# Low-query passes on 128 rows instead of 64, in two attentions and a memory attention

## The chip, the cores and the metric

The kernel runs on 1 core of a Trainium2 chip. The metric is device time in microseconds (us) of one execution; lower is better. TensorE (PE) multiplies: its weight loads are told as PEld and overlap with its matmuls. VectorE (DVE), ScalarE (ACT) and GpSimd (POOL) do the rest; SyncE (SP) issues every DMA here.

## The reference

A trunk of two layers on a sequence of 1024 positions of width 1024, all in float32. Cut to what the change touches:

```python
for layer in range(2):
    h = rms_norm(x, mix_norm_g[layer])
    da_q, da_k, da_v, sb_q, sb_k, sb_v, c_q, c_kv, k_r = split(h @ w_in[layer])
    y_a = diff_attention(...)     # 4 heads; per head two softmaxes over 64-wide q and k, plus a bias
    y_b = stick_breaking(...)     # 4 heads of 64
    y_c = latent_attention(...)   # 4 heads of 64 + 32
    x = x + concatenate([y_a, y_b, y_c]) @ w_out[layer]
    x = x + memory_attention(rms_norm(x), mem, ...)   # 4 heads of 64 over 256 memory tokens
    x = x + square(relu(rms_norm(x) @ w_ff1[layer])) @ w_ff2[layer]
```

In each of these attentions the scores of a head are `q @ k.T`, with q and k 64 wide (96 in the latent attention), and masked so that a query sees its own block and those before it.

## The kernel before

*Precision.* Matmuls run in a reduced float32 (`F32R`). An operand is therefore split into a high part (rounded to that format) and a low part (what is left), and a product is made of passes: high x high, high x low, low x high. In the projections, `mm3` (L572 to L575) issues three matmuls for each block.

*Rows.* A matmul sums over rows, at most 128. Where a head is 64 wide, two of those passes fit in one matmul: the keys' tile `ks` has the high keys in rows 0 to 63 and the low keys in rows 64 to 127 (`stack`, L961), and the queries' tile `qh` has the high queries twice (`twice`, L975). One pass of 128 rows so gives high x high + high x low. The low queries `ql` lie on 64 rows (`block`, L969), and the second pass takes rows 0 to 63 of both: low x high. Latent heads (96 wide) have three passes of 96 or 100 rows.

*Attention.* `attention(h, ...)` (L940) does one half of the queries: h = 0 are the tiles 0 to 3 of 128 queries, with up to 512 keys; h = 1 are the tiles 4 to 7, with up to 1024. For each of the 4 heads of a kind, the tiles of queries and keys are loaded from scratch in DRAM by `dma` on SP's queue, then for each tile of queries `scores` (L989) issues the passes: each over the keys in pieces of at most 512 columns, one bank of PSUM. Half 0 has one piece a pass (PSUM tile `e`), half 1 has two (PSUM tile `d`). In a differential head (`da_head`, L1066) there are two such score blocks a tile of queries, and each has two more matmuls that add the bias through a permutation (`flip`). Query tiles and biases share the ring of tiles named `o` (6 or 7 of them), keys are in `kst`, values in `v`. After the scores come a row maximum (L1091), exponentials, or sigmoids and a scan (L1121) in the stick-breaking heads, transposes through PE (L594) and the products with the values (L1027, L1042, L1044).

*Memory attention.* It is part of `merge` (L1156), once for each half of the queries and each layer. Its keys `km` are stacked high over low on 128 rows; the queries, transposed and present on both halves of the rows, are split into `qT[:, 0]` (high, L1188) and `qT[:64, 1]` (low, L1189). For each of 4 heads there is one pass of 128 rows (L1200) and one of 64 (L1201), 256 columns each.

*Order.* The program isn't run as written. `order_engines` (L223) plans all of it: it takes each instruction when its inputs are there by a model of costs (`_cost`, L191: a matmul by its columns; a DMA 450 ns on SP and its bytes on the DMA engines), by rank (`mem.rank`), and fixes the order on each engine. So projections of one half lie among the first half's attention, and the MLP of the first half (`ff1`, `ff2`; L1266) among the attention and `merge` of the second. Every weight block is loaded as `raw` and split by ScalarE (L551) and VectorE (L552).

Of the kernel before, what the change touches and what calls it, by code (L numbers as in the profile page):

```python
# [17 lines left out]
P = 128  # L18
# [324 lines left out]
def trunk(ctx: ExitStack, mem: Mem, tc: tile.TileContext, a: dict, out: bass.AP):  # L343
    nc = tc.nc
    HT = NT // 2
    HS = S // 2
# [8 lines left out]
    def f(ap):  # L355
        return ap.bitcast(F32)
# [290 lines left out]
    for l in range(L):  # L647
        R = 100 * l
        names = ("q", "k")
        dqk = [[[dp.tile([4 * P, HS], F32, tag=f"dqk{l}{h}{j}{g}") for g in range(2)] for j in names] for h in range(2)]  # L650
# [289 lines left out]
        def attention(h, ap_):  # L940
# [125 lines left out]
            def da_head(d):  # L1066
                g, r = d // 2, (d % 2) * P
                ks, qh, ql, bt = [], [], [], []
                for m in range(2):
                    r0 = r + m * 64  # L1070
                    ks.append(stack([dqk[u][1][g] for u in range(h + 1)], r0, 2 * P + r0, 64))
                    qh.append(twice(dqk[h][0][g], r0, 64))
                    ql.append(block([dqk[h][0][g]], 2 * P + r0, 64, "o", bufs["o"], HS))
                    b = ap_.tile([P, HS], F32R, tag="o", bufs=bufs["o"]).rearrange("p (s k) -> p s k", s=2)
                    dma(f(b), biasd[2 * d + m])
                    bt.append(b)
                vt = values(dv, d * P, F32)
                for t in tiles(h):
                    n = (t + 1) * P
                    cq = slice((t % HT) * P, (t % HT + 1) * P)  # L1080
                    sm = small()
                    pm = []
                    for m in range(2):
                        adds = []
                        for s in range(2):
                            if t == 0:
                                adds.append((flipR, bt[m][:, s, 128:], 0, 128))
                            else:
                                adds.append((flipR, bt[m][:, s, :], n - 256, 256))
                        ps = scores(t, [(qh[m][:, cq], ks[m]), (ql[m][:64, cq], ks[m][:64])], adds)  # L1090
                        nc.vector.tensor_reduce(sm[:, m:m + 1], ps[:, :n], axis=AX.X, op=ALU.max, negate=True)  # L1091
                        pt = ptile()
                        nc.scalar.activation(pt[:, :n], ps[:, :n], AF.Exp, bias=sm[:, m:m + 1],
                                             accum_out=sm[:, 2 + m:3 + m])
                        pm.append(pt)
                    nc.vector.reciprocal(sm[:, 4:6], sm[:, 2:4])
                    nc.vector.scalar_tensor_tensor(sm[:, 6:7], sm[:, 2:3], sm[:, 5:6], neglam[:, l:l + 1],
                                                   op0=ALU.mult, op1=ALU.mult)
                    nc.vector.scalar_tensor_tensor(pm[0][:, :n], pm[1][:, :n], sm[:, 6:7], pm[0][:, :n],
                                                   op0=ALU.mult, op1=ALU.add)  # L1100
                    po = weighted(t, pm[0], vt)
                    nc.scalar.activation(y[t][:, d * P:(d + 1) * P], po, AF.Copy, scale=sm[:, 4:5])
                    norm_y(t, d * P, P, sm[:, 7:8], rows3[0])

            def sb_head(d):
                g, r = d // 2, (d % 2) * 64
                ks = stack([sqk[u][1][g] for u in range(h + 1)], r, P + r, 64)
                qh = twice(sqk[h][0][g], r, 64)
                ql = block([sqk[h][0][g]], P + r, 64, "o", bufs["o"], HS)
                vs = values(sv, d * P, F32R)  # L1110
                for t in tiles(h):
                    n = (t + 1) * P
                    cq = slice((t % HT) * P, (t % HT + 1) * P)
                    ps = scores(t, [(qh[:, cq], ks), (ql[:64, cq], ks[:64])], [])
                    om, be = ptile(), ptile()
                    nc.scalar.activation(om[:, :n], ps[:, :n], AF.Sigmoid, scale=-0.125)
                    nc.scalar.activation(be[:, :n], ps[:, :n], AF.Sigmoid, scale=0.125)
                    dg = slice(n - P, n)
                    nc.vector.tensor_tensor(om[:, dg], om[:, dg], before[:, 1, :], op=ALU.max)
                    nc.gpsimd.tensor_tensor(be[:, dg], be[:, dg], before[:, 0, :], op=ALU.mult)  # L1120
                    nc.vector.tensor_tensor_scan(om[:, :n][:, ::-1], om[:, :n][:, ::-1],  # L1121
                                                 zero1.to_broadcast([P, n]), 1.0, op0=ALU.mult, op1=ALU.add)
                    nc.gpsimd.tensor_tensor(be[:, :n - 1], be[:, :n - 1], om[:, 1:n], op=ALU.mult)
                    c = 512 + d * 64
                    weighted64(t, be, vs, y[t][:, c:c + 64], 1.0)
                    norm_y(t, c, 64, small()[:, 7:8], rows3[1])
# [29 lines left out]
        def merge(h, cls, km, vm, gx, gf):  # L1156
# [27 lines left out]
            for t in tiles(h):  # L1184
                pt = bank(cls)
                transposes(pt, qds[t % HT], 4)
                qT = t4().rearrange("p (s c) -> p s c", s=2)
                nc.scalar.activation(qT[:, 0, :], pt, AF.Copy, scale=gq)  # L1188
                nc.vector.scalar_tensor_tensor(qT[:64, 1, :], pt[:64, :], gq[:64, :], f(qT[:64, 0, :]),  # L1189
                                               op0=ALU.mult, op1=ALU.subtract)  # L1190
                sm = stat()
                po = None
                pm = f(t4())
                for hh in range(2):
                    ps = bank(cls)
                    for i in range(2):
                        d = 2 * hh + i
                        o_ = ps[:, i * 256:(i + 1) * 256]
                        cq = slice(d * P, (d + 1) * P)
                        nc.tensor.matmul(o_, qT[:, 0, cq], km[:, d, :], start=True, stop=False)  # L1200
                        nc.tensor.matmul(o_, qT[:64, 1, cq], km[:64, d, :], start=False, stop=True)  # L1201
                    nc.vector.tensor_reduce(sm[:, 2 * hh:2 * hh + 2], ps.rearrange("p (h k) -> p h k", h=2), axis=AX.X,
                                            op=ALU.max, negate=True)
                    for i in range(2):
                        d = 2 * hh + i
                        nc.scalar.activation(pm[:, d * 256:(d + 1) * 256], ps[:, i * 256:(i + 1) * 256], AF.Exp,
                                             bias=sm[:, d:d + 1], accum_out=sm[:, 4 + d:5 + d])
                nc.vector.reciprocal(sm[:, 8:12], sm[:, 4:8])
                om = f(t2())
                at = f(t4())  # L1210
                for hh in range(2):
                    pt = bank(cls)
                    transposes(pt, pm[:, hh * 512:], 4)
                    nc.scalar.activation(at[:, hh * 512:(hh + 1) * 512], pt, AF.Copy)
                po = bank(cls)[:, :256]
                for d in range(4):
                    for j in range(2):
                        s = slice((2 * d + j) * P, (2 * d + j + 1) * P)
                        nc.tensor.matmul(po[:, d * 64:(d + 1) * 64], at[:, s], vm[:, j, d, :], start=j == 0, stop=j == 1)
                nc.vector.tensor_tensor(om[:, :256].rearrange("p (h d) -> p h d", h=4),  # L1220
                                        po.rearrange("p (h d) -> p h d", h=4),
                                        sm[:, 8:12].unsqueeze(2).to_broadcast([P, 4, 64]), op=ALU.mult)
                pt = bank(cls)[:, :256]
                transposes(pt, om, 2)
                oT = t2().rearrange("p (s c) -> p s c", s=2)
                split(pt, oT[:, 0, :], oT[:, 1, :])
                for c in range(2):
                    cc = slice(c * 512, (c + 1) * 512)
                    px = bank(cls)
                    for k in range(2):  # L1230
                        s = slice(k * P, (k + 1) * P)
                        mm3(px, oT[:, 0, s], oT[:, 1, s], wmo[k][c][0], wmo[k][c][1], k == 0, k == 1)
                    nc.vector.tensor_tensor(xt[t][:, cc], px, xt[t][:, cc], op=ALU.add)
                norm_T(xt[t], gf, *h_at(hT, t), cls)
# [201 lines left out]
```

## Time and profile before

| | |
|---|---|
| median of 3 runs | 3046.2 us (3042.35 to 3048.5) |
| profiled execution | 3053.11 us, span 3051.3 us |
| PE busy | 2978.9 us (98%) |
| PEld busy | 2519.0 us (83%) |
| DVE busy | 1941.2 us (64%) |
| ACT busy | 1404.2 us (46%) |
| POOL busy | 464.0 us (15%) |
| DMA moved | 348.04 MB, mean 114 GB/s |
| mean granted clock of TensorE | 0.993 |

The span goes from the first to the last instruction; the execution's own time has a little around it. Busy times are means over stages that differ: in the projections and the MLP, PE works without a pause, in the attentions several engines take turns. Matmuls are pipelined, and a profile models their ends; the starts of neighbours tell what one costs. In a row such as `64*128 64x512`, the first pair is rows x columns of the weights, the second rows x columns of what streams through. The part named "idle before" at a row's end tells what the engine waited for.

### The profile page before, as it was taken

The page shows a single profiled execution, that of the slowest core. Times are in us where ns is not written, and L with a number is a line of the kernel's source. Part 1 is how long each engine was busy: PE and PEld are TensorE (multiplying, and loading weights), DVE is VectorE, ACT ScalarE, POOL GpSimd, SP SyncE. Part 2 cuts the span into 40 slices and gives each one's busy share as a digit, 9 for nine tenths or more (in the row PEclk, how much of TensorE's full clock was granted, in tenths as well). Part 3 has the DMA queues.
Part 4 walks back from the last instruction along what each step waited for, and adds up shares of the span by engine and source line. Part 5 has one row for each costly group of instructions (what it writes and reads, how often), then busy time and mean ns, then how long its engine had stood idle before and what let it go on. Part 6 is the DMA issues. An engine that isn't in the chain of part 4 may idle for free.

```text
span 3051.3 us, 46379 instructions
## 1 busy us (share of the span) xinstructions
PE 2978.9 (98%) x16818; PEld 2519.0 (83%) x16818; DVE 1941.2 (64%) x3715; ACT 1404.2 (46%) x3330; POOL 464.0 (15%) x556
## 2 busy tenths in 40 slices
PE   8999999999999999999999999999999999999999
PEld 7977988677898888888899779886788988888887
DVE  6777675876757544465567875758767565444555
ACT  5666555655635322133345664556656443222232
POOL 1352131420101000000013521314101000000000
PEclk9999999999999999999999999999999999999999
DMA  7755534633232211123257564345342411111222
GB/s 238 225 170 178 166 100 122 166 104 117 76 123 66 70 56 42 42 85 107 89 171 215 157 192 143 105 128 141 116 121 69 126 56 49 56 56 42 97 93 90
DMA packets 377365, 348.04 MB, mean 114 GB/s; under 512 B 26600, under 2 KB 300432, under 8 KB 377136
## 3 DMA queue, kind: packets, MB, share of 16 engines
q1 hardware_dynamic: 377136, 345.08, 37.4%
q8 instruction: 133, 2.18, 0.3%
q14 instruction: 96, 0.79, 0.1%
HBM read 284.10 MB, written 60.88 MB: 113 GB/s over the span
## 4 chain that ended last, share of the span: by engine, by line
PE 74%; DVE 4%; DMA 3%; ACT 2%; POOL 2%; issue 1%; SPq 1%; DVEq 0%; ACTq 0%; POOLq 0%
PE d L1266 17%; PE s L575 10%; PE s L573 10%; PE s L574 10%; PE s L1266 6%; PE d L1007 4%; PE s L594 3%; PE s L1027 2%; PE s L1042 1%; PE e L574 1%; PE e L575 1%; PE e L573 1%; PE e L1007 1%; DMA raw<-in_w_out 1%; DVE w L552 1%
## 5 line engine op out<-in xcount | busy, mean ns | idle before, releaser
L551 ACT ACTIVATE w<-raw 128x512 fp32r<-128x512 f32 (+1 forms) x688 | 421.3, 627 | 568.7 <-PE d L1266 244.9
L552 DVE TENSOR_TENSOR w<-raw,w 128x512 fp32r<-128x512 f32 (+1 forms) x688 | 469.2, 693 | 198.8 <-ACT w L551 196.8
L573 PE MATMUL s<-h,w 128*128 128x512 f32 x1120 | 446.7, 399 | 0.5 <-ACT w L551 0.5
L575 PE MATMUL s<-h,w 128*128 128x512 f32 x1120 | 446.9, 399 | 0.0
L574 PE MATMUL s<-h,w 128*128 128x512 f32 x1120 | 444.6, 397 | 0.0
L1270 DVE TENSOR_TENSOR x<-d,x 128x1024 f32<-128x1024 f32 (+1 forms) x185 | 225.1, 1217 | 169.8 <-PE d L1266 169.8
L581 POOL TENSOR_TENSOR ms<-ms,mhalf 128x4 f32<-128x4 f32 (+3 forms) x144 | 147.1, 1024 | 1150.8 <-DVE ms L579 1148.8
L573 PE MATMUL s<-w,h 128*128 128x256 f32 (+1 forms) x1024 | 299.3, 296 | 9.6 <-ACT h L586 3.6
L574 PE MATMUL s<-w,h 128*128 128x256 f32 (+1 forms) x1024 | 299.3, 295 | 1.8 <-DVE w L552 1.8
L575 PE MATMUL s<-w,h 128*128 128x256 f32 (+1 forms) x1024 | 298.0, 293 | 0.3 <-DVE h L587 0.3
L1266 PE MATMUL d<-w,hid 128*128 128x512 f32 x1152 | 267.0, 389 | 0.0
L1243 ACT ACTIVATE r<-s 128x512 f32<-128x512 f32 x128 | 76.4, 597 | 400.7 <-issue 233.0
L1245 DVE TENSOR_TENSOR r<-r 128x512 f32<-128x512 f32 x128 | 95.3, 745 | 256.0 <-ACT r L1243 255.7
L1266 PE MATMUL s<-w,hid 128*128 128x512 f32 x864 | 250.9, 411 | 4.9 <-ACT w L551 3.7
L1266 PEld LDWEIGHTS d<-w,hid 128*128 128x128 f32 x1152 | 216.2, 188 | 45.6
L1266 PE MATMUL d<-w,t 128*128 128x512 f32 x1056 | 248.5, 393 | 0.0
L575 PEld LDWEIGHTS s<-h,w 128*128 128x128 f32 x1120 | 210.8, 188 | 44.8 <-DVE w L552 0.6
L574 PEld LDWEIGHTS s<-h,w 128*128 128x128 f32 x1120 | 210.9, 188 | 43.3 <-issue 1.7
L573 PEld LDWEIGHTS s<-h,w 128*128 128x128 f32 x1120 | 210.9, 188 | 43.0 <-issue 1.5
L1266 PEld LDWEIGHTS d<-w,t 128*128 128x128 f32 x1056 | 198.7, 188 | 44.9
L1063 POOL TENSOR_TENSOR sm<-sm,mhalf 128x1 f32<-128x1 f32 x192 | 132.1, 688 | 590.8 <-DVE sm L1062 450.7
L573 PEld LDWEIGHTS s<-w,h 128*128 128x128 f32 x1024 | 192.8, 190 | 14.6 <-ACT h L586 4.2
(337 smaller groups left out, 6048.7 us busy)
## 6 DMA issues: line engine op xcount, KB each, us to landing
raw<-in_w_ff SPq DMA_DIRECT2D x400, 256.0 KB
raw<-in_w_in SPq DMA_DIRECT2D x144, 256.0 KB
raw<-in_w_out SPq DMA_DIRECT2D x64, 256.0 KB
x<-in_x SPq DMA_DIRECT2D x16, 512.0 KB
o<-biasd SPq DMA_DIRECT2D x32, 256.0 KB
raw<-in_w_in SPq DMA_DIRECT2D x32, 208.0 KB
v<-sv SPq DMA_DIRECT2D x24, 256.0 KB
v<-mv SPq DMA_DIRECT2D x24, 256.0 KB
```

The costliest lines, as they stand in the source:

```text
L551: nc.scalar.activation(w[:, 0, o], raw, AF.Copy)
L552: nc.vector.tensor_tensor(w[:, 1, o], raw, f(w[:, 0, o]), op=ALU.subtract)
L573: nc.tensor.matmul(ps, sh, mh, start=start, stop=False)
L574: nc.tensor.matmul(ps, sh, ml, start=False, stop=False)
L575: nc.tensor.matmul(ps, sl, mh, start=False, stop=stop)
L581: nc.gpsimd.tensor_tensor(rs, ms, mhalf[:, :n], op=ALU.pow)
L594: nc.tensor.transpose(ps[:, k * P:(k + 1) * P], src[:, k * P:(k + 1) * P], ident)
L1007: nc.tensor.matmul(ps[:, c:c + w], sta, mov, start=first, stop=last[c // 512] == i)
L1063: nc.gpsimd.tensor_tensor(sm, sm, mhalf[:, :1], op=ALU.pow)
L1245: nc.vector.tensor_tensor(r2, r, r, op=ALU.mult)
L1266: nc.tensor.matmul(parts[e], hd[i][:, s, tt], w[:, e * 512:(e + 1) * 512], start=first, stop=last)
L1270: nc.vector.tensor_tensor(xt[t][:, cols], ps, xt[t][:, cols], op=ALU.add)
```

## The change

The low queries are loaded twice, on rows 0 to 63 and 64 to 127, by two DMAs of 64 rows where there was one, and their pass takes all 128 rows of the keys' tile: it gives low x high + low x low. In the memory attention the low queries are computed on all 128 partitions (the transposed queries are on both halves already), and their pass takes 128 rows as well. Columns, tiles, banks and the number of matmuls stay as they are.

```diff
 # da_head
-                    ql.append(block([dqk[h][0][g]], 2 * P + r0, 64, "o", bufs["o"], HS))
+                    ql.append(twice(dqk[h][0][g], 2 * P + r0, 64))
...
-                        ps = scores(t, [(qh[m][:, cq], ks[m]), (ql[m][:64, cq], ks[m][:64])], adds)
+                        ps = scores(t, [(qh[m][:, cq], ks[m]), (ql[m][:, cq], ks[m])], adds)
...
 # sb_head
-                ql = block([sqk[h][0][g]], P + r, 64, "o", bufs["o"], HS)
+                ql = twice(sqk[h][0][g], P + r, 64)
...
-                    ps = scores(t, [(qh[:, cq], ks), (ql[:64, cq], ks[:64])], [])
+                    ps = scores(t, [(qh[:, cq], ks), (ql[:, cq], ks)], [])
...
 # merge
-                nc.vector.scalar_tensor_tensor(qT[:64, 1, :], pt[:64, :], gq[:64, :], f(qT[:64, 0, :]),
+                nc.vector.scalar_tensor_tensor(qT[:, 1, :], pt, gq, f(qT[:, 0, :]),
                                                op0=ALU.mult, op1=ALU.subtract)
...
-                        nc.tensor.matmul(o_, qT[:64, 1, cq], km[:64, d, :], start=False, stop=True)
+                        nc.tensor.matmul(o_, qT[:, 1, cq], km[:, d, :], start=False, stop=True)
```

## The prediction

> **What bounds the kernel now.** I read the page first: the shares by engine, the granted clock, the chain that ended last.
>
> ```profile
> span 3051.3 us, 46379 instructions
> PE 2978.9 (98%) x16818; PEld 2519.0 (83%) x16818; DVE 1941.2 (64%) x3715; ACT 1404.2 (46%) x3330; POOL 464.0 (15%) x556
> PEclk9999999999999999999999999999999999999999
> PE 74%; DVE 4%; DMA 3%; ACT 2%; POOL 2%; issue 1%; SPq 1%; DVEq 0%; ACTq 0%; POOLq 0%
> ```
>
> TensorE (PE) is busy nearly all the time, at full clock. The chain's shares add up to 87% of the span (it is lost before 407 us), and 74 of the 87 are PE. So whatever PE does less of comes off the end, except where the chain runs over another engine. A busy PE isn't PE at its peak, though: the ends of matmuls are modelled. What a matmul occupies is read from the starts of its neighbours. So next I listed the groups by shape, to see what the diff's instructions are now.
>
> ```profile
> L1007 PE MATMUL d<-kst,o 64*128 64x512 f32 x96 | 43.5, 479 | 0.0
> L1007 PE MATMUL d<-kst,o 64*128 64x384 f32 x48 | 17.4, 362 | 0.0
> L1007 PE MATMUL d<-kst,o 64*128 64x256 f32 x48 | 16.2, 338 | 0.2 <-DMA o<-sqk01q 0.2
> L1007 PE MATMUL e<-kst,o 64*128 64x512 f32 x24 | 11.9, 495 | 0.0
> ...
> L1007 PE MATMUL e<-kst,o 64*128 64x128 f32 x24 | 8.1, 336 | 0.1
> L1201 PE MATMUL d<-km,t 64*128 64x256 f32 x16 | 6.1, 382 | 0.0
> ```
>
> `64*128` is 64 rows by 128 columns of weights. In the second half's attention (tile d) there are 192 such matmuls, two pieces to a pass, so 96 passes; in the first half's (tile e) 4 groups of 24, one piece each, 96 passes; in the memory attention four groups of 16, 64 passes. 256 passes in all, and nothing else in the kernel but one set-up matmul has so few rows. Their mean durations tell little (pipelined), so I went to the order of time, in a stretch where the memory attention's passes lie among ordinary ones of the same 256 columns. The first column is the start.
>
> ```profile
> 468.89 0.28 PE L574 MATMUL s<-w,h 128*128 128x256 f32 x1
> 469.00 0.28 PE L575 MATMUL s<-w,h 128*128 128x256 f32 x1
> 469.12 0.28 PE L573 MATMUL s<-w,h 128*128 128x256 f32 x1
> 469.33 0.38 PE L1201 MATMUL e<-km,x 64*128 64x256 f32 x1
> 469.64 0.39 PE L1200 MATMUL e<-km,x 128*128 128x256 f32 x1
> 469.95 0.38 PE L1201 MATMUL e<-km,x 64*128 64x256 f32 x1
> 470.26 0.38 PE L574 MATMUL s<-w,h 128*128 128x256 f32 x1
> 470.49 0.28 PE L575 MATMUL s<-w,h 128*128 128x256 f32 x1
> 470.60 0.28 PE L573 MATMUL s<-w,h 128*128 128x256 f32 x1
> ```
>
> Two matmuls of 128 rows start 0.12 us apart. Going into a 64-row pass takes 0.21, out of it 0.31, and the interval after that is still long (470.26 to 470.49, 0.23). From 469.12 to 470.60 there are six intervals and two such passes: 1.48 us where six times 0.118 is 0.71. Excess 0.77, that is 0.385 us a pass, with nobody waited for. Is it the 64 rows, or merely rows that aren't 128? The latent heads use 96 rows. Here are four pieces (256 and 384 columns, twice) of a head with a 64-row pass, and further down the same four pieces with 96 rows throughout.
>
> ```profile
> 632.76 0.94 PE L1007 MATMUL d<-kst,o 128*128 128x256 f32 x4
> 633.62 0.50 PE L1007 MATMUL d<-o,flip 128*128 128x256 f32 x2
> 633.97 0.40 PE L573 MATMUL s<-h,w 128*128 128x512 f32 x1
> ...
> 751.83 0.75 PE L1007 MATMUL d<-kst,o 96*128 96x256 f32 x4
> 752.42 1.05 PE L1027 MATMUL s<-v,t 128*128 128x128 f32 x8
> ```
>
> The 96-row four take 0.59 us from start to next start, the four with two 64-row pieces 0.86, and the two bias matmuls after those 0.35 where 2 x 0.118 is 0.24. Excess 0.27 + 0.11 = 0.38 again: a pass in two pieces pays once. So a price of 0.385 us hangs on each turn to 64 rows and back.
>
> **The change part by part.** *The 256 passes.* Their columns stay, their rows become 128, the weights of the pass before have 128 rows too, so no turn is left. 256 x 0.385 = 98.6 us of PE time goes (a little more where the planner put another matmul between two pieces of a pass, which then pays twice). The low-times-low products ride along for nothing: 0.59 us for 96 rows and 0.12 for 128 rows per 256 columns show no price of rows as such. How much of the 98.6 is on the path? I asked for the chain by line in five stretches: a memory attention of each half, the second half's attention in both layers, and the first half's in layer 1.
>
> ```profile
> by line: PE s L574 16.6%; PE s L575 16.1%; PE s L573 16.1%; PE e L594 9.2%; PE s L1219 7.8%; PE s L594 5.4%; PE e L573 3.7%; PE e L575 3.7%; PE s L1201 3.7%; PE e L574 3.7%; PE e L1219 3.2%; PE s L1200 3.1%; PE e L1201 2.5%; ACT x L1214 2.4
> by line: PE s L1266 22.3%; PE s L575 13.4%; PE s L574 11.9%; PE s L573 11.9%; PE s L594 8.1%; PE d L1219 5.8%; PE d L1201 5.3%; PE d L574 4.0%; PE d L575 4.0%; PE d L1200 4.0%; PE d L594 3.8%; PE d L573 3.3%; PE s L1201 1.8%; PE s L1200 1.2
> by line: PE d L1007 20.1%; PE s L1266 12.8%; PE s L1027 8.6%; PE s L594 7.1%; DVE t L1121 5.4%; PE s L573 4.5%; PE s L575 4.3%; PE s L574 4.3%; PE s L1042 3.6%; issue 3.5%; SPq L966 2.4%; DVE r L1245 1.9%; PE s L1051 1.9%; POOL t L1120 1.8%
> by line: PE d L1007 24.6%; PE s L1266 16.3%; PE s L1027 11.5%; PE s L594 7.8%; DVE t L1121 4.3%; PE s L573 3.7%; PE s L575 3.5%; PE s L574 3.5%; issue 3.1%; PE s L1042 2.9%; DVE w L552 2.0%; PE s L1051 1.9%; POOL t L1120 1.8%; POOL t L1123
> by line: PE e L1007 19.1%; PE s L575 6.3%; PE s L573 6.2%; PE s L574 6.1%; PE s L594 5.7%; PE s L1027 4.0%; PE s L1044 3.3%; issue 3.1%; DMA mv<-t 2.8%; PE e L574 2.6%; DVE w L552 2.5%; DVE p L1121 2.5%; DMA o<-biasd 2.5%; DMA raw<-in_w_in
> ```
>
> PE's parts add up to 95% and 100% in the memory attentions (I take 97%), 67% and 76% in the second half's attention (71%), and 53% of what is shown in the first half's; its small groups are cut off, so I take 60%, and the same for layer 0, where the chain is lost. The sum: 64 x 0.385 = 24.6, of which 23.9; 96 x 0.385 = 37.0, of which 26.4; 37.0 again, of which 22.2. Together 72.5 us. The bounds: all 98.6, if the engines that PE waits for in between were themselves let loose by the earlier matmuls; 24.6 alone, if the attentions turned out to be bound by the others altogether.
>
> *The extra loads.* Each low-query tile now takes two DMAs of 64 rows instead of one: 2 a differential head, 1 a stick-breaking head, over 4 heads, 2 halves, 2 layers: 32 + 16 = 48 more, of 128 KB each, 6.3 MB on 348. All are issued by SP's queue, in order. The queue at the start of the second half's attention in layer 1, and the chain there (2033 to 2075 us):
>
> ```profile
> 2045.22 1.08 SPq L966 DMA_DIRECT2D kst<-sqk11k  x2
> 2046.40 1.18 SPq L978 DMA_DIRECT2D o<-sqk11q  x2
> 2047.62 0.59 SPq L972 DMA_DIRECT2D o<-sqk11q  x1
> 2048.26 1.14 SPq L985 DMA_DIRECT2D v<-sv  x2
> ...
> by line: SPq L966 21.0%; DMA dv<-t 16.2%; PE d L1007 10.1%; DMA dqk11q<-t 8.4%; DMA raw<-in_w_ff 7.6%; DMA o<-sqk11q 6.5%; PE s L573 4.9%; PE s L575 4.9%; PE s L574 4.9%; DVE t L1121 4.8%; SPq L978 4.1%; issue 3.4%; ACT t L795 2.8%; PE s L5
> ```
>
> An issue costs SP 0.59 us, so 48 cost 28.3 us of its time: the upper bound if every one delayed the end; nothing, if each lies in a pause of the queue. Behind each stand the value loads, the next head's keys and a weight load, and the queue is on the chain for 25% here (21.0 + 4.1). At such a start six more issues come in a row (four stick-breaking heads, the first differential one): 6 x 0.59 = 3.5 us, four times 14.2, and at 25% some 4 us on the path. The later heads' loads go out as tiles come free, well ahead of use, and cost nothing while that lead lasts. A second wait, for the second DMA, stands before the low pass alone; behind it on PE stand the bias matmuls and the row maximum.
>
> In the Trainium skill, "DMA: Bandwidth & Descriptors", section "Rules for kernel authors", two transfers to disjoint partition halves are advised against, for one of 128 partitions, since both use the same 16 engines; that speaks against this edit's form, and by it the 48 loads buy no bandwidth. No run here shows the single transfer.
>
> *The subtraction in the memory attention* (VectorE, 16 of them) takes 128 partitions instead of 64.
>
> ```profile
> L1189 DVE SCALAR_TENSOR_TENSOR x<-e,gcol,x 64x512 fp32r<-64x512 f32 x4 | 3.0, 743 | 1.3 <-ACT x L1188 1.3
> L1099 DVE SCALAR_TENSOR_TENSOR p<-p,sm,p 128x512 f32<-128x512 f32 x8 | 6.0, 750 | 0.2
> ```
>
> 743 ns at 64 partitions, 750 at 128 in the nearest row: 16 x 7 ns, nothing.
>
> *The planned order.* The kernel computes its engine order from costs in which a matmul's price comes from its columns alone, so the passes do not move; the 48 DMAs do enter, and may swap neighbours. The trace can't price that. In the four attention stretches PE is idle for 830.0 - 796.4 = 33.6 us by this row:
>
> ```profile
> sum 830.00, PE 796.42 PEld 640.44 DVE 620.76 ACT 508.88 POOL 253.70; mean PE 199.10 PEld 160.11 DVE 155.19 ACT 127.22 POOL 63.42
> ```
>
> A better order could win at most that, a worse one may lose as much; I take 0. The same row gives VectorE 75% there: room, but it is late next, with the scan (L1121) and the row maxima.
>
> Sum: 72.5 - 4 = 68.5 us, from the span of 3051.3 to 2983 (the profiled execution took 3053.1 with what lies around it). The median of the runs is 3046.2, so **2978 us**.
>
> **The rivals.** *All of it:* PE's saving passes through in full, 98.6, and the loads hide: 3046 - 99 = 2947. For: PE 98% busy. Against: a third of the attention's chain is not PE's.
> *Absorbed:* the attentions wait for softmax chains and loads as soon as PE is faster, and what remains is the memory attention and a third of the rest: 23.9 + 16 - 4 = 36, 3010. For: 4 to 5% of the chain in the second half's attention on the scan, the DMAs in the last row of the five. Against: the idle PE time is only 4% there.
> *The rows set nothing:* the long intervals come from the order or the tiles, and remain: 3046 + 4 = 3050. Against: the 96-row four at 0.59 us, in the same tiles. The Trainium skill's "TensorE: Matmul & The Clock Gate", section "Why this matters for your kernels", has it that a matmul on 32 rows takes as long as one on 128, which by itself makes this change worth nothing; the rows at 469 us disagree (0.31 against 0.12). "TensorEngine Tiling (Array Packing)", section "Key Properties", says that changing the tiling mode drains the engine, and agrees with them.
> *Slower, by SP's queue:* the attention's pace is set by the loads, PE's savings there are lost in waits, and every issue comes on top. Then 24.6 us are won, and from (24.6 + 6) / 48 = 0.64 us an issue the kernel is slower. The 0.59 us seen falls just short; if crowding doubled it, to 1.18, 57 - 24.6 = 32 us are lost: 3078. Against: outside the starts SPq is 2.4% of the chain at most in the rows above.
>
> **How the numbers follow.** Within 0.2%, 6 us, a measurement of this kernel cannot tell a change from none (the three runs shown lie 6.2 us apart). Chances: the likeliest 0.72 (2951 to 3001 by itself), all of it 0.09, absorbed 0.12, no effect 0.03, slower 0.04. The predicted time is that of the first, 2978. The range 2940 to 3012 holds the first two and a part of the third. Faster 0.93, same 0.03, slower 0.04.
>
> **What would show it.** In the profile after: no `64*128` group is left; L1200 and L1201 start 0.12 us apart; PE's idle time in the attention stretches grows by the share that isn't passed on (about 26 us); the memory attentions shrink by 6 us each; 48 more loads on SP, each near 0.59 us. Wrong would be: PE waits on `o` tiles at the heads' starts of over 10 us in all, an order that leaves PE uncovered in the attention, or a granted clock below the present one.

## The result, and the profile after

2971.7 us (median of 4 runs, 2966.2 to 2974.9) against 3044.6 before (a fourth run moved that median from 3046.2): ratio 0.9757, 95% interval 0.9738 to 0.9777, that is 73 us or 2.4% less. Predicted were 68 us less. The two profiled executions lie 87 us apart: before's took 3053.1, more than any of the four runs timed with it, and after's is the fastest of its four. So shares of the gain are told from medians, and the profiles are used for where and how.

The page of after: span, busy times by engine, the chain's shares by engine.

```profile
span 2964.5 us, 46467 instructions
PE 2880.0 (97%) x16818; PEld 2507.9 (85%) x16818; DVE 1933.8 (65%) x3715; ACT 1399.8 (47%) x3330; POOL 464.1 (16%) x556
PE 79%; DVE 7%; DMA 5%; issue 3%; ACT 3%; POOL 3%; SPq 1%; DVEq 0%; POOLq 0%; ACTq 0%
```

The same 16818 matmuls keep PE busy for 98.9 us less (2978.9 - 2880.0), where the sum had 98.6. PE's idle time rose from 72.4 to 84.5 us. The groups of after by shape:

```profile
L1007 PE MATMUL d<-kst,o 128*128 128x512 f32 x192 | 69.8, 422 | 0.3 <-ACT t L1117 0.2
L1007 PE MATMUL d<-kst,o 128*128 128x384 f32 x96 | 32.6, 348 | 0.0
L1200 PE MATMUL e<-km,x 128*128 128x256 f32 x16 | 4.4, 284 | 0.0
L1201 PE MATMUL e<-km,x 128*128 128x256 f32 x16 | 4.2, 282 | 0.0
```

High and low passes of a shape now stand in one group, 192 with 512 columns instead of 96 and 96. The order of time on PE shows two places that answer to those of before: eight passes of the memory attention, and the four pieces (256 and 384 columns, twice) with their two bias matmuls.

```profile
425.94 0.28 PE L575 MATMUL e<-w,x 128*128 128x256 f32 x1
426.06 0.29 PE L1200 MATMUL s<-km,x 128*128 128x256 f32 x1
426.19 0.28 PE L1201 MATMUL s<-km,x 128*128 128x256 f32 x1
426.30 0.28 PE L1200 MATMUL s<-km,x 128*128 128x256 f32 x1
426.42 0.28 PE L1201 MATMUL s<-km,x 128*128 128x256 f32 x1
...
427.02 0.82 PE L594 MATMUL e<-ident,t 128*128 128x128 f32 x6
...
612.89 0.75 PE L1007 MATMUL d<-kst,o 128*128 128x256 f32 x4
613.47 0.40 PE L1007 MATMUL d<-o,flip 128*128 128x256 f32 x2
613.71 0.39 PE L573 MATMUL s<-h,w 128*128 128x512 f32 x1
```

Every pass starts 0.12 us after the last, in place of 0.21 and 0.31; no `64*128` group is left on the list. The four pieces take 0.58 us instead of 0.86, the bias matmuls 0.24 instead of 0.35: 0.82 where it was 1.21.

### The profile page after: what moved, and what is told of

Read it like the earlier page. It is cut to its first block, busy times and chain, and to the rows that moved or that the text cites. A ratio compares the mean times of both kernels' runs of the same rounds, so it can differ in the third digit from the quotient of the medians.

```text
span 2964.5 us, 46467 instructions
## 1 busy us (share of the span) xinstructions
PE 2880.0 (97%) x16818; PEld 2507.9 (85%) x16818; DVE 1933.8 (65%) x3715; ACT 1399.8 (47%) x3330; POOL 464.1 (16%) x556
## 4 chain that ended last, share of the span: by engine, by line
PE 79%; DVE 7%; DMA 5%; issue 3%; ACT 3%; POOL 3%; SPq 1%; DVEq 0%; POOLq 0%; ACTq 0%
PE d L1266 17%; PE s L575 12%; PE s L574 12%; PE s L573 12%; PE s L1266 5%; PE s L594 4%; PE d L1007 3%; PE s L1027 2%; PE e L1007 2%; PE e L573 2%; PE e L575 2%; PE e L574 2%; DVE t L1121 1%; DMA raw<-in_w_in 1%; PE s L1042 1%
```

## The experiments

All ratios are to runs of before on the same chip, taken in the same session; differences in us between experiments are differences of such ratios times before's time. The whole change had 0.9757. Where two kernels are said to have the same order on an engine, their traces show the same instructions one after the other.

### The price of the turn, by itself

Three kernels put the disputed cost into the MLP's first product of after, where PE waits for nobody.

```diff
# mlp_one: the second pass of row block 6 (of 0 to 7) in ff1; mlp_two: the second and the third; mlp_96: the second, with [:96]
-  nc.tensor.matmul(ps, sh, ml, start=False, stop=False)
+  nc.tensor.matmul(ps, sh[:64], ml[:64], start=False, stop=False)
```

> After, with the price measured by itself where PE waits for nobody: in the MLP's first product, one of the 24 passes of each block (the second of the seventh row block) takes 64 rows instead of 128, which leaves out half of that partial product. 128 such passes in all, planned order as after's on every engine. Theory 1 (a turn costs 0.385 us): 128 x 0.385 = 49 us, all on the path: 2972 + 49 = 3021, ratio 0.992. Rival (rows set nothing): 2972, ratio 0.976.

> The same with two neighbouring passes on 64 rows, of different weights: 256 passes, 128 turns. Theory 1 (the price is that of the turn, and is paid once for the two): 3021, ratio 0.992. Rival (the price is that of each pass of 64 rows): 2972 + 99 = 3071, ratio 1.008.

> The same as the first with 96 rows instead of 64: 128 passes that aren't of 128 rows. Theory 1 (96 rows need no turn): 2972, ratio 0.976. Rival (any change of the number of rows costs): 3021, ratio 0.992.

Measured: mlp_one 0.990 (0.988 to 0.992), mlp_two 0.9918 (0.9898 to 0.9939), mlp_96 0.9749 (0.9731 to 0.9768). Against after's 0.9757, the one pass costs 44 us in 128 places, 0.34 each; two neighbours cost 49, no more than one does within the intervals (in 16 of the 128 places another matmul lies between the two, so there are 144 turns, again 0.34 each); 96 rows cost nothing. The order of time on PE in mlp_one, mlp_two and mlp_96 (line 576 holds the three passes of the edited row block):

```profile
2990.23 0.40 PE L575 MATMUL s<-h,w 128*128 128x512 f32 x1
2990.47 1.24 PE L576 MATMUL s<-h,w 128*128 128x512 f32 x3
2991.54 0.40 PE L573 MATMUL s<-h,w 128*128 128x512 f32 x1
2991.78 0.39 PE L574 MATMUL s<-h,w 128*128 128x512 f32 x1
```

```profile
2991.67 1.04 PE L576 MATMUL s<-h,w 128*128 128x512 f32 x3
2992.64 0.50 PE L573 MATMUL s<-h,w 128*128 128x512 f32 x1
2992.98 0.39 PE L574 MATMUL s<-h,w 128*128 128x512 f32 x1
```

```profile
2941.12 0.87 PE L576 MATMUL s<-h,w 128*128 128x512 f32 x3
2941.83 0.40 PE L573 MATMUL s<-h,w 128*128 128x512 f32 x1
2942.07 0.39 PE L574 MATMUL s<-h,w 128*128 128x512 f32 x1
```

With 96 rows the three take 0.71 us to the next start; with one of 64 rows 1.07; with two 0.97, and the matmul after them is late by another 0.11 (2992.64 to 2992.98, 0.34 for 0.23). Excess 0.36 and 0.37. So the price does not go by the number of 64-row passes, and 96 rows have none: what costs is going to 64 rows and coming back. What holds PE up shows in the idle time of the weight loads before this line, mlp_one:

```profile
L576 PEld LDWEIGHTS s<-h,w x384: 182/186/192, 511.2 to 2991.2; 128*128 128x128 f32 x128, 64*128 64x128 f32 x64
its engine sat idle before it (us, times) until:
  issue: 70.4, 236
```

In 236 places the weight load stood idle for 0.30 us (70.4 / 236) although nothing was waited for; in mlp_96 that list is empty. So at a turn the next weights are loaded late. In the Trainium skill, "TensorEngine Tiling (Array Packing)", section "Key Properties", says that changing the tiling mode drains the engine; these rows agree with that, and add the price. That a pass of 64 rows is another tiling mode in the page's sense is not shown by any run here.

A last kernel leaves before's rows and passes as they are, and brings passes of a kind together.

```diff
-  for i in range(2):                     # per head: high pass (128 rows), low pass (64 rows)
-      matmul(o_, qT[:, 0, cq], km[:, d, :], start=True, stop=False)
-      matmul(o_, qT[:64, 1, cq], km[:64, d, :], start=False, stop=True)
+  for s in range(2):                     # both heads' high passes, then both low passes
+      for i in range(2):
+          ...
```

> Before, with the memory attention's passes in another order: for the two heads of a bank first both passes of 128 rows, then both of 64. All rows as in before; 64 passes of 64 rows, but 32 turns. The planned order moves little otherwise. Theory 1 (price per turn): 32 x 0.385 = 12.3 us less: 3034, ratio 0.996. Rival (price per pass): 3046, ratio 1.000.

Measured: 0.9970 (0.9957 to 0.9983), 9 us less (5 to 13) for 32 turns. The rival's 1.000 is outside the interval, theory 1's 12.3 inside. The planner also moved matmuls in 164 other places of TensorE's 16818 (the change itself moved 3060), and that was not priced apart. With this said, half of the memory attention's turns can be saved without touching a row.

### The change in parts

```diff
# mem_only: before with
+  nc.vector.scalar_tensor_tensor(qT[:, 1, :], pt, gq, ...)
+  nc.tensor.matmul(o_, qT[:, 1, cq], km[:, d, :], start=False, stop=True)
# att_only: after without these two
# loads_only: att_only, and the passes back on 64 rows
-  (ql[:, cq], ks)
+  (ql[:64, cq], ks[:64])
```

> Before, with the memory attention's part of the change alone (64 low passes on 128 rows); the planned order of TensorE is that of before, instruction by instruction. Theory 1 (each turn to 64 rows and back costs 0.385 us): 64 x 0.385 = 24.6 us, of which 97% on the path: 3044.6 - 24 = 3021, ratio 0.992. Theory 2 (the gain comes from the new planned order): 3045, ratio 1.000. L1200 and L1201 start 0.12 us apart under theory 1.

> After, with the memory attention put back to 64 rows; the planned order is that of after on every engine. Theory 1: the rest of the gain measured, 73 - 24 = 49 us less than before: 2996, ratio 0.984. Theory 2 (order): all of it, 2972, ratio 0.976.

> Before, with the 48 extra loads alone: low queries are loaded on both halves of the rows, all low passes take 64 rows as before. The planner is told to wait for both loads, so that the planned order is that of after on TensorE, ScalarE, GpSimd and SP. Theory 1: the loads cost 4 us (0 to 28): 3049, ratio 1.001. Theory 2 (order): most of the 49 us that the attentions won is here: 3000, ratio 0.985. Theory 3 (SP's queue sets the pace of the attention): +28 us, 3073, ratio 1.009.

Measured: mem_only 0.9932 (0.9916 to 0.9949), att_only 0.9824 (0.9807 to 0.9842), loads_only 0.9975 (0.9965 to 0.9985). The memory attention's rows win 21 us on an unchanged order of TensorE; theory 2 falls for them. att_only and loads_only have the same order on every engine and the same loads, so the attentions' rows win 0.9975 - 0.9824 = 1.51%, 46 us. But loads_only was expected at 3049 by theory 1 and came out 7.5 us *faster* than before: 48 loads more and nothing else but another planned order. That lies between theory 1 and theory 2 (3000) and fits neither; the next kernels split it.

### The loads and the planned order

The planner sees the extra loads and orders all engines anew. Three kernels separate the two: the loads without their effect on the plan, the plan without the loads, and the whole change on the old plan.

```diff
# loads_oldplan (64 rows) and after_oldplan (128 rows): in order_engines, for the second load of ql
+  cost[x] = 0.0; dmab[x] = 0
# before_newplan: before, with a twin of each load of ql in the plan alone (same inputs, cost, bytes and users)
+  preds.append(set(preds[x])); cost.append(cost[x]); dmab.append(dmab[x]); ...
+  order[4] = [x for x in order[4] if x < real]
```

> Before, with the 48 extra loads (low queries on both halves, passes on 64 rows), and the planner told that each extra load is free, so that the order on TensorE, VectorE, ScalarE and GpSimd is that of before, instruction by instruction. The run with the loads and the changed order was 7.5 us faster than before. Theory 1 (the loads cost about 4 us, the changed order wins some 11): 3050, ratio 1.001. Rival (the loads win by themselves): 3039, ratio 0.9975.

> Before, with one load for each low-query tile and all low passes on 64 rows, but planned as if there were two: TensorE, VectorE, ScalarE and GpSimd have after's order of instructions, nothing else is changed. It is the fourth corner beside before (old order, one load), the loads with the old order (+0.49%) and the loads with the new order (-0.25%). Theory 1 (the new order wins by itself, about 22 us, and the loads cost about 15 on either order): 3024, ratio 0.993. Rival (the old order only fits the loads badly; without the extra loads the orders are alike): 3046, ratio 1.000.

> After, with the extra loads free for the planner, so that the compute engines keep the order of before. Theory 1 (rows and order add up): the rows' 22 + 47 us are won, the loads cost 4, the order's 11 are missing: 2981, ratio 0.979. Rival (the order wins nothing, or belongs to the rows): as after, 2972, ratio 0.976.

Measured, with 64 rows everywhere:

| | order of before | order of after |
|---|---|---|
| one load | 1 (before) | 0.9924 (0.9908 to 0.9941) |
| two loads | 1.0049 (1.0035 to 1.0063) | 0.9975 (0.9965 to 0.9985) |

Neither expectation for loads_oldplan (1.001 and 0.9975) fits; theory 1 for before_newplan (0.993) does. The loads cost 0.49% on the old order and 0.51% on the new, 15 us; the new order wins 0.76% with one load and 0.74% with two, 23 us. after_oldplan had 0.9859 (0.9844 to 0.9874): on 128 rows the old order is worse by 1.0%, 31 us, and the rows alone win 1.9% on it (1.0049 to 0.9859), 58 us, instead of 2.2% on the new one (0.9975 to 0.9757), 66 us. Theory 1's sum (0.979) missed after_oldplan by 0.7%. About half of that is the loads, which it had at 4 us instead of 15. The other half is the rows, 58 us where it had 69; whether rows and order really fail to add up is open, since 1.9% and 2.2% differ by no more than the intervals of the four ratios allow.

The page of before_newplan gives 55.1 us of idle time on PE, where before had 72.4:

```profile
span 3029.2 us, 46370 instructions
PE 2974.1 (98%) x16818; PEld 2518.1 (83%) x16818; DVE 1940.0 (64%) x3715; ACT 1404.3 (46%) x3330; POOL 464.9 (15%) x556
```

That is 17 of the 22 us by which the two profiled spans differ. About half of the 17 lies in the stretches of the first half's attention of layer 0 and of what follows it (160 to 350, 350 to 530 us), here before and then before_newplan; the numbers are busy us of PE, PEld, DVE, ACT and POOL:

```profile
160.00:350.00 190.00, 180.75 (x1079) 149.80 (x1078) 144.66 (x422) 127.67 (x419) 66.84 (x95) 0.96 0.59 177
350.00:530.00 180.00, 175.17 (x1357) 165.55 (x1357) 112.39 (x233) 87.52 (x205) 36.12 (x39) 1.00 0.38 112
```

```profile
160.00:350.00 190.00, 185.05 (x1116) 154.87 (x1116) 148.24 (x429) 128.97 (x423) 67.22 (x96) 0.96 0.61 183
350.00:530.00 180.00, 179.32 (x1359) 168.21 (x1358) 113.69 (x231) 90.08 (x206) 39.01 (x41) 1.00 0.41 119
```

PE is idle there for 5.6 us instead of 14.1, with 39 more matmuls done. Shown is that the order wins, and that most of it is PE's idle time. Which of the many changed neighbours do it was not tried.

### One load of 128 rows

If the loads cost by their issues, fewer of them must win. The rows of keys and queries are interleaved (2r high, 2r + 1 low for the keys; the two query rows are alike), and one DMA fills all 128.

```diff
 # stack
-  for o, r in ((0, r0), (rows, r1)):
-      dma(f(k[o:o + rows, u * HS:(u + 1) * HS]), src[u][r:r + rows])
+  s = src[u][r0:r0 + rows]
+  dma(f(k[:, u * HS:(u + 1) * HS]),
+      bass.AP(tensor=s.tensor, offset=s.offset, ap=[[HS, rows], [(r1 - r0) * HS, 2], [1, HS]]))
 # twice: the same with [0, 2] in the middle
 # after_oneplan: after, its second loads free in the plan and the first ones double in bytes
```

> After, with the rows of the stick-breaking and differential keys and queries interleaved (row 2r high, 2r + 1 low; both query rows alike), so that one DMA of 128 rows fills a tile or half of it where two of 64 rows did: 168 DMAs fewer, the same bytes. Theory 1: the issues on SP are a small part of the path; what the 48 cost (about 4 us) comes back, and up to 14 us by the ratio of counts: 2958 to 2968, ratio 0.972 to 0.975. Rival (an issue costs by its rows): as after, 2972, ratio 0.976.

> After with its pairs of loads of 64 rows, but planned as if the second of each pair were free, so that the compute engines have the order of the version with one load of 128 rows (18 us faster than after). Theory 1 (fewer issues on SP are what won): as after, 2972, ratio 0.976. Theory 2 (the planned order won): 2954, ratio 0.970. In between, it is split in that proportion.

Measured: one_load 0.9697 (0.9679 to 0.9716), 2953.8 us, 18 us less than after, more than theory 1's range had (2958 to 2968), and the fastest of all kernels here; after_oneplan, with one_load's order on the compute engines and after's loads, 0.9761 (0.9746 to 0.9776), as after. So it is the 168 fewer loads that won, at the same bytes, and not the order of the compute engines. PE's waits for loads into `o`, added up over one traced execution of each, are 16.6 us in after_oneplan and 6.8 in one_load. SP's queue at the start of the second half's attention in layer 1, in after and then in one_load:

```profile
1976.35 2.46 SPq L978 DMA_DIRECT2D o<-sqk11q  x4
1978.85 1.14 SPq L985 DMA_DIRECT2D v<-sv  x2
1980.08 1.10 SPq L966 DMA_DIRECT2D kst<-sqk10k  x2
1981.22 1.23 SPq L966 DMA_DIRECT2D kst<-sqk11k  x2
1982.50 2.51 SPq L978 DMA_DIRECT2D o<-sqk11q  x4
```

```profile
1966.03 1.22 SPq L979 DMA_DIRECT2D o<-sqk11q  x2
1967.29 1.14 SPq L986 DMA_DIRECT2D v<-sv  x2
1968.53 0.52 SPq L966 DMA_DIRECT2D kst<-sqk10k  x1
1969.09 0.60 SPq L966 DMA_DIRECT2D kst<-sqk11k  x1
1969.74 1.25 SPq L979 DMA_DIRECT2D o<-sqk11q  x2
```

A stick-breaking head's loads take 6.15 us of the queue in after (1976.35 to 1982.50) and 3.71 in one_load. An issue of 128 rows costs what one of 64 does, 0.5 to 0.6 us, at twice the bytes. The Trainium skill's advice in "DMA: Bandwidth & Descriptors", "Rules for kernel authors", to use one transfer of 128 partitions rather than two of halves, holds here; what these rows show to be saved is SP's time to issue. Whether the loads also land sooner was not measured.

## Why the prediction was right, point by point

- *0.385 us a turn, 256 passes, 98.6 us of PE.* Right: the rows at 426 and 613 us, 0.34 to 0.37 by itself in the MLP, and PE's busy time down by 98.9. That the two figures meet within 0.3 us is luck: before's trace has 276 turns, not 256, since the planner put other matmuls between the two pieces of some passes, and the profiles differ in granted clock (0.993 and 0.995).
- *72.5 of it on the path, by the chain's shares.* Nearly right: 21 us in the memory attention (23.9 foretold; some 5 us for each of the four, where 6 were named), 46 in the attentions on one and the same order (48.6). The first half's 60%, where the chain was lost or cut off, was not measured apart from the second's. What is not passed on turns up as idle time of PE, as foretold (26 us): from loads_only, which has after's loads and order, to after it grew by 27 us over the whole span, from 57.4 to 84.5. The page of loads_only:

```profile
span 3034.2 us, 46425 instructions
PE 2976.8 (98%) x16818; PEld 2523.9 (83%) x16818; DVE 1940.5 (64%) x3715; ACT 1404.2 (46%) x3330; POOL 464.1 (15%) x556
```

- *The loads, 4 us (0 to 28).* Mis-sized: 15 us, on either order. The step that failed is what the sum let through: a quarter of the 24 issues at the attentions' starts, by SP's share in one stretch of the second half's chain, and nothing of the later heads' 24. Measured is a loss of 15, about half of the 28.3 us of issue time. Part of it is seen in the first half's attention (tile e), from which the quarter was not read. PE's waits before a score matmul there, before and then after:

```profile
L1007 PE MATMUL e<-kst,o 128*128 128x128 f32 x24 | 6.6, 275 | 2.1 <-DMA o<-sqk00q 1.5 <-DMA o<-sqk10q 0.6
L1007 PE MATMUL e<-kst,o 128*128 128x128 f32 x48 | 12.5, 294 | 9.5 <-DMA o<-dqk10q 3.0 <-DMA o<-dqk00q 2.5 <-DMA o<-sqk00q 1.6
```

All of PE's waits for loads into `o` are 3.3 us in before and 10.7 in after, just beyond the 10 us that the prediction named as a sign of being wrong. The loads alone raise them by 2.6 us (from before_newplan, 2.0, to loads_only, 4.6) or by 4.8 (from before, 3.3, to loads_oldplan, 8.1). Where the rest of the 15 goes, and whether it is due to the issues or to the 6.3 MB, is open: an issue is worth 15 / 48 = 0.31 us by the 48 loads and 18 / 168 = 0.11 us by one_load.

- *The planned order, 0 (at most 33.6 either way).* The bound was right, the value was not: 23 us won, 17 of them seen as idle time of PE. The bound had been read from PE's idle time in the four attention stretches.
- *The sum.* That 68.5 came so close to 73 is in part luck: the rows were 5.5 us too high, the loads 11 too cheap, and the order's 23 were missing, errors that partly cancel. By the parts measured: 21 + 46 - 15 + 23 = 75.
- *The subtraction on 128 partitions*, costed at nothing: right. Line 1189 takes 748 ns (median) in after and 742 in before, and mem_only, which holds it, still wins 21 of 23.9.
- *The rivals.* "The rows set nothing" fell by mlp_one. "All of it" and "absorbed" fell by the parts: 67 us of rows came through, between the 40 of "absorbed" (23.9 + 16) and the 98.6. "Slower, by SP's queue" needed 0.64 us an issue on the path; 15 / 48 = 0.31 were paid.
- *PE's idle time* from before to after grew by 12 us over the whole span, not by 26: the rows added 27 and the loads 2, and the new order took 17 away (profiles of before, before_newplan, loads_only, after: 72.4, 55.1, 57.4, 84.5).

## What to carry to other kernels

A matmul on 64 rows among matmuls of more rows was not cheaper here but dearer: 0.34 to 0.385 us for going there and back, paid once for one or for two such passes in a row; so fill the rows, even with terms nobody needs, or bring such passes together. Read the price of a matmul from its neighbours' starts, not from its duration. And where an order is planned from costs, any added instruction is two changes: measure it with the plan held fixed, and the plan without it, before either is believed.

## What the runs showed of the hardware that was not expected

Two loads of 64 rows cost SP's queue twice what one of 128 rows of twice the bytes does (0.5 to 0.6 us each), and 168 fewer loads at the same bytes won 18 us in a kernel whose TensorE is busy 97% of the time. The 48 loads more, with 6.3 MB, lost 15. Passes of 96 rows, unlike those of 64, ran among those of 128 at no price that could be measured (0.9749 against 0.9757).
